# Other durations in the estimate by which a decoder-layer kernel orders its TensorE work

## The chip, the cores and the metric

The kernel runs on one core of one Trainium2 chip. The metric is device time of one execution in microseconds (us), the median of three runs. The engines are PE (TensorE, with PEld for its weight loads), DVE (VectorE), ACT (ScalarE), POOL (GpSimd) and SP (SyncE), which here only issues DMAs.

## The reference, cut to what matters

One decoder layer on x of 2048 tokens by 1024 channels, all in float32. D_FF is 2816.

```python
h = rms_norm(x, attn_norm)
dn_qkv, dn_z, dn_b, dn_a, sq, sk, sv, gate_raw = split_combined(h @ w_in)
y_dn = gated_deltanet_branch(dn_qkv, dn_z, dn_b, dn_a, ...)    # 4 heads of 128, a state carried along the tokens
y_swa = sliding_window_branch(sq, sk, sv, ...)                 # 8 query heads of 64, window 128
gates = sigmoid(gate_raw)
merged = gates[0] * (y_dn @ w_branch_dn) + gates[1] * (y_swa @ w_branch_swa)
x = x + merged @ w_out
h2 = rms_norm(x, ffn_norm)
x = x + (silu(h2 @ w_gate) * (h2 @ w_up)) @ w_down
```

Inside the first branch each chunk of tokens needs a unit triangular solve and then a step of the recurrence `S = g S + k_dec^T v_new`, so chunk follows chunk.

## The kernel before, in words

The tokens go in four blocks of 512 (`NB = 4`). A block passes through a *mixer* (projections of the delta-rule heads, gates, both branches, merge), then the output projection, then the feed-forward part. The products with weights are the **dense** work. Each is done as three matmuls (`mm3`, `tok_mm`, lines 194 and 208): both factors are split into a high and a low part of type float32r, and high x high, high x low and low x high are added in PSUM. One such triple is called a **group** below; its matmuls write tiles named `acc`. All else is **side** work: small matmuls and transposes into tiles named `aux`, with chains of operations on DVE, ACT and POOL between them. Products of the delta rule are plain float32 matmuls.

PE's order is written out by hand (`manual_schedule` for PE alone, line 1034); the framework orders the other engines by itself, side work with raised priority (line 243). `drive` (line 217) emits it: the dense work is one generator, and each side chain is a generator in `self.sides`. After every group `drive` looks for a side chain whose *due* time has come by an estimated clock `est.now`, and emits its next step, that is, the step's matmuls and what follows them on the other engines up to the next `yield`. A side step's new due time is the estimated end of the operations it emitted plus HOP + SLACK, 220 + 30 ns (line 250).

The estimate is `Estimate.note` (line 72). Every emitted operation gets a start, the latest of `est.now`, the engine's own free time, and the ready times of its inputs plus HOP (220 ns, an input made on the same engine included), and an end by a formula for its engine and size (lines 78 to 85). A matmul advances `est.now` to its end; operations on the other engines only move that engine's free time. One call of `matmul` or `transpose` is priced once. `n` is the number of columns for PE and the largest number of elements per partition for the others. `bank` (line 68) holds a side step back until the oldest of eight PSUM banks is estimated free. The splitting of weights into high and low parts (`weights`, line 155; done in block 0 only, kept in DRAM for the rest) is emitted past the estimate.

When the dense generator yields a condition, `drive` emits side steps alone, in order of their due times, until the condition holds (line 229). One such place is in `mixer`: after the gates and `branch` for all eight m, `yield lambda: len(ydn) == NH` (line 986) holds back `merge` until the last delta-rule head is done.

The four heads run in two lanes (`dn_cores`, line 710): heads 0 and 2 in one, 1 and 3 in the other. `dn_core` (line 716) of one head and block has these steps: `gu` on POOL; the decay matrix, 8 plain products and the DVE chain to `be` (lines 729 to 772); a loop of 30 small DVE operations that solves 16 x 16 blocks (line 780; the *solver loop*), which ends in `R`; two levels of three steps and three more steps that widen the solve to 128; then four chunks of three *scan steps* (lines 831 to 851, tiles `vb`, `wv`, `state` and `O`); then the norm of the output (lines 853 to 860, with 14 small DVE operations on tile `dst`; the *last wait*), the transposes of `O`, and `ydn`. When `branch` is emitted, `norm1` of the next block is started as another side chain (line 983).

Of the kernel before, what the change touches and what calls it, by code (L numbers as in the profile page):

```python
# [56 lines left out]
class Estimate:  # L57
# [14 lines left out]
    def note(self, eng, name, args, kw):  # L72
        aps = [(k, a) for k, a in list(enumerate(args)) + list(kw.items()) if hasattr(a, "tensor")]
        outs = [a for k, a in aps if k in ("out", "accum_out", 0) and (k or "out" not in kw)]
        ins = [a for k, a in aps if not any(a is o for o in outs)]
        n = max(int(np.prod([d[1] for d in list(a.ap)[1:]])) for _, a in aps)
        start = max([self.now, self.free.get(eng, 0.0)] + [self.ready.get(a.tensor.name, 0.0) + HOP for a in ins])
        if eng == "tensor":
            n = int(np.prod([d[1] for d in list(outs[0].ap)[1:]]))
            f32 = any(a.dtype == F32 for a in ins)  # L80
            end = start + max(n / 2.4 * (1 if not f32 else 2 if name == "transpose" else 4), 107 if f32 or n > 64 else 53)
            self.now = end
        else:
            end = start + {"vector": 70 + n / 0.96, "scalar": 160 + n / 1.4, "gpsimd": 100 + n * 2.2}[eng]
            self.free[eng] = end
            self.done = max(self.done, end)
        for a in outs:
            self.ready[a.tensor.name] = end
        for a in outs + ins:
            if a.tensor.name in self.banks or eng == "tensor" and a is outs[0]:  # L90
                self.seq += 1
                self.banks[a.tensor.name] = (self.seq, end)
                if len(self.banks) > 8:
                    self.banks.pop(min(self.banks, key=lambda k: self.banks[k][0]))
# [1034 lines left out]
```

## Time and profile before

| | |
|---|---|
| runs | 3184.16, 3185.84, 3180.29 us |
| median | 3184.16 us |
| profiled execution, its own time | 3183.98 us |
| its span, first to last instruction | 3182.2 us |
| granted TensorE clock over the span | 0.991 of full |
| PE busy | 3088.4 us, 97% |
| DVE, ACT, POOL busy | 44%, 26%, 13% |
| plain 512-column float32r matmul, start to start in a run of 30 | 0.235 us |

Matmul ends are modelled and matmuls overlap, so durations of single PE records are longer than what each adds; the distance from start to start tells the cost. A plain float32 matmul of the program leaves two records on PE, a float32r one or a transpose leaves one: the program has 64 calls that write `aux` from `wv` and `kd`, and the trace has 128 records of them.

### The profile page before, as it was taken

How to read it: one execution, taken by the hardware profiler on the slowest of the kernel's cores; microseconds unless marked ns; L12 is line 12 of the kernel's file. 1: busy time of each engine (PE TensorE's matmuls, PEld its weight loads, DVE VectorE, ACT ScalarE, POOL GpSimd, SP SyncE). 2: the span in 40 equal slices, each digit the busy share in tenths (PEclk: the TensorE clock that was granted, in tenths of full speed). 3: DMA queues.
4: the chain of work that ended last, by engine and by line, in shares of the span. 5: the costliest groups of instructions: out<-in, count | busy, mean ns of one | idle time of the engine just before them, and what ended most of it. 6: DMA issues, size and time to landing. Idle time of an engine off the chain costs nothing. (4 is left out here: it accounts for less than half of the span.)

```text
span 3182.2 us, 39714 instructions
## 1 busy us (share of the span) xinstructions
PE 3088.4 (97%) x14854; PEld 2520.7 (79%) x14854; DVE 1401.6 (44%) x3599; ACT 834.3 (26%) x2106; POOL 409.6 (13%) x395
## 2 busy tenths in 40 slices
PE   7889999999999999999999999999999999999999
PEld 6667778788888888778887888877888888878887
DVE  6876656533346544532216465353211655422121
ACT  4444434523323322320002323141000233110000
POOL 1423212322221100010002010011000211000000
PEclk9989999999999999999999999999999999999999
DMA  7445576688874456445566445545656544555555
GB/s 263 157 146 188 190 264 202 197 284 283 284 240 139 133 162 205 151 156 188 185 192 196 135 140 183 176 155 165 196 188 207 165 131 131 197 162 194 190 188 184
DMA packets 291848, 595.99 MB, mean 187 GB/s; under 512 B 18975, under 2 KB 20168, under 8 KB 291656
## 3 DMA queue, kind: packets, MB, share of 16 engines
q1 hardware_dynamic: 277072, 568.15, 54.4%
q10 hardware_dynamic: 14584, 25.30, 2.3%
q8 instruction: 117, 1.92, 0.2%
q14 instruction: 75, 0.61, 0.1%
HBM read 459.08 MB, written 134.30 MB: 186 GB/s over the span
## 5 line engine op out<-in xcount | busy, mean ns | idle before, releaser
L109 PE MATMUL acc<-h,whl 128*128 128x512 f32 x7296 | 1761.9, 397 | 6.2 <-DVE QE L109 6.2
L109 PEld LDWEIGHTS acc<-h,whl 128*128 128x128 f32 x7296 | 1355.8, 189 | 309.2 <-DVE QE L109 6.4
L109 PE MATMUL acc<-whl,a 128*128 128x512 f32 x2112 | 493.7, 393 | 0.0
L109 PEld LDWEIGHTS acc<-whl,a 128*128 128x128 f32 x2112 | 395.5, 188 | 90.3
L109 DVE TENSOR_TENSOR x<-x,acc 128x512 f32<-128x512 f32 x192 | 131.2, 687 | 391.3 <-PE acc L109 388.7
L173 POOL TENSOR_TENSOR whl<-wraw,whl 128x512 fp32r<-128x512 f32 x117 | 159.2, 1361 | 589.7 <-ACT whl L170 544.4
L170 ACT ACTIVATE whl<-wraw 128x512 fp32r<-128x512 f32 (+1 forms) x240 | 149.4, 629 | 295.2 <-PE acc L109 169.6
L109 DVE TENSOR_TENSOR th<-th,acc 128x512 f32<-128x512 f32 x88 | 60.4, 687 | 315.8 <-PE acc L109 315.5
L109 DVE SCALAR_TENSOR_TENSOR th<-th,acc 128x512 f32<-128x512 f32 x88 | 60.4, 687 | 307.8 <-ACT th L109 307.8
L109 PE MATMUL acc<-whl,mt 128*128 128x512 f32 x768 | 181.6, 398 | 5.4 <-DVE h L109 4.6
L109 ACT ACTIVATE th<-acc 128x512 f32<-128x512 f32 x88 | 52.6, 598 | 501.5 <-PE acc L109 501.4
L109 PEld LDWEIGHTS acc<-whl,mt 128*128 128x128 f32 x768 | 146.2, 191 | 40.1 <-DVE h L109 5.1
L109 DVE SCALAR_TENSOR_TENSOR cv<-xr,cst_sb,cv 128x512 f32<-128x512 f32 x144 | 134.4, 933 | 57.1 <-ACT cv L109 52.5
L109 ACT ACTIVATE a<-th 128x512 fp32r<-128x512 f32 x88 | 55.5, 631 | 346.7 <-DVE th L109 332.1
L173 DVE TENSOR_TENSOR whl<-wraw,whl 128x512 fp32r<-128x512 f32 (+1 forms) x123 | 94.0, 765 | 106.9 <-ACT whl L170 102.5
L109 PE MATMUL acc<-whl,h 128*128 128x264 f32 (+1 forms) x768 | 139.0, 340 | 0.0
L109 PEld LDWEIGHTS acc<-whl,h 128*128 128x128 f32 x768 | 118.0, 188 | 15.6
L109 POOL COPY ccar<-xr 128x3 f32<-128x3 f32 x48 | 9.7, 203 | 847.1 <-ACT xr L109 847.0
L109 PE MATMUL acc<-sp,whl 128*128 128x512 f32 x384 | 101.3, 405 | 0.0
L109 POOL TENSOR_TENSOR pT<-pT,cst_sb 128x512 f32<-128x512 f32 x62 | 81.9, 1351 | 130.2 <-ACT pT L109 114.2
L109 ACT ACTIVATE L<-L,ast 128x256 f32<-128x256 f32 (+1 forms) x192 | 83.5, 458 | 52.6 <-DVE ast L109 52.4
L109 PE MATMUL acc<-ydn,whl 128*128 128x512 f32 x384 | 92.2, 399 | 0.4
(186 smaller groups left out, 2808.4 us busy)
## 6 DMA issues: line engine op xcount, KB each, us to landing
whl<-wk SPq DMA_DIRECT2D x708, 512.0 KB, 3.9
wk<-whl SPq DMA_DIRECT2D x236, 512.0 KB, 3.7
wraw<-in_w_all SPq DMA_DIRECT2D x118, 512.0 KB, 4.9
x<-in_x ACTq DMA_DIRECT2D x60, 256.0 KB, 5.3
out<-x ACTq DMA_DIRECT2D x32, 256.0 KB, 3.1
whl<-wk SPq DMA_DIRECT2D x12, 528.0 KB, 4.7
wk<-whl SPq DMA_DIRECT2D x4, 528.0 KB, 4.6
wraw<-in_w_skv SPq DMA_DIRECT2D x2, 528.0 KB, 5.8
```

The lines of the kernel that those rows point to most:

```text
L109: r = f(*args, **kw)
L170: nc.scalar.activation(hi, r, AF.Copy)
L173: eng.tensor_tensor(out=lo, in0=r, in1=hi, op=ALU.subtract)
```

## The change

Four formulas of `Estimate.note` are replaced: PE's (float32r and float32, with matmul and transpose of float32 no longer told apart) and those of DVE, ACT and POOL. HOP, SLACK and everything else stay. No instruction is added or removed; what can differ is the order on PE, and with it the order that the framework gives the other engines.

```diff
         if eng == "tensor":
             n = int(np.prod([d[1] for d in list(outs[0].ap)[1:]]))
             f32 = any(a.dtype == F32 for a in ins)
-            end = start + max(n / 2.4 * (1 if not f32 else 2 if name == "transpose" else 4), 107 if f32 or n > 64 else 53)
+            end = start + (max(n * 0.452, 60) if not f32 else max(n * 0.87, 60))
             self.now = end
         else:
-            end = start + {"vector": 70 + n / 0.96, "scalar": 160 + n / 1.4, "gpsimd": 100 + n * 2.2}[eng]
+            end = start + {"vector": 155 + n * 1.04, "scalar": 150 + n * 0.92, "gpsimd": 100 + n * 2.45}[eng]
             self.free[eng] = end
             self.done = max(self.done, end)
```

In ns, by these formulas:

| operation | before | after |
|---|---|---|
| group of three 512-column float32r matmuls | 640 | 694 |
| float32 transpose, 128 columns | 107 | 111 |
| plain float32 matmul, 128 columns, one call | 213 | 111 |
| DVE, 512 elements | 603 | 687 |
| DVE, 4 elements | 74 | 159 |
| ACT, 512 elements | 526 | 621 |
| ACT, 128 elements | 251 | 268 |
| POOL, 512 elements | 1226 | 1354 |

## Rows read from the trace of the kernel before

**Rows 1.** The page, first part: busy us, share of the span, instructions.

```profile
PE 3088.4 (97%) x14854; PEld 2520.7 (79%) x14854; DVE 1401.6 (44%) x3599; ACT 834.3 (26%) x2106; POOL 409.6 (13%) x395
```

**Rows 2.** Windows of four stretches; columns in the first line.

```profile
core 0: us, PE busy (x) PEld busy (x) DVE busy (x) ACT busy (x) POOL busy (x), PEclk, DMA share, GB/s
0.00:410.00 410.00, 349.13 (x1818) 283.51 (x1819) 283.81 (x780) 184.60 (x498) 122.35 (x113) 0.95 0.55 188
1184.00:1958.00 774.00, 767.05 (x3717) 627.41 (x3715) 319.64 (x867) 173.98 (x466) 62.12 (x69) 1.00 0.53 171
393.25:405.70 12.45, 3.10 (x19) 2.34 (x18) 9.23 (x41) 6.87 (x23) 1.44 (x1) 0.67 0.47 152
1206.00:1217.00 11.00, 8.68 (x48) 7.33 (x47) 10.54 (x19) 5.97 (x10) 0.00 (x0) 0.84 0.71 221
```

**Rows 3.** Waits of PE, 80 to 410 us: us in total, times, longest.

```profile
PE aux L109 <- ACT T L109: 15.8, 3, 9.8
PE aux L109 <- DVE O L109: 9.0, 2, 7.6
```

**Rows 4.** Waits of PE, 500 us to the end, same columns.

```profile
PE aux L109 <- DVE be L109: 6.7, 9, 0.9
...
PE acc L109 <- DVE h L109: 4.6, 2, 2.3
```

**Rows 5.** PE at the end of block 1's mixer: start, us, operation.

```profile
1176.82 7.20 PE L109 MATMUL acc<-sp,whl 128*128 128x512 f32 x30
1183.86 0.60 PE L109 MATMUL aux<-cst_sb,O 128*128 128x128 f32 x4
```

**Rows 6.** Groups of operations: count | busy us, mean ns | idle before.

```profile
L109 DVE TENSOR_TENSOR x<-x,acc 128x512 f32<-128x512 f32 x192 | 131.2, 687 | 391.3 <-PE acc L109 388.7 <-DMA whl<-wk 2.1
...
L109 PE MATMUL aux<-state,cv 128*128 128x128 f32 x256 | 39.4, 277 | 0.6 <-DVE state L109 0.6
...
L109 PE MATMUL aux<-cst_sb,cv 128*128 128x128 f32 x192 | 29.6, 278 | 2.9 <-DVE cv L109 2.9
...
L109 DVE SCALAR_TENSOR_TENSOR dst<-dst 128x4 f32<-128x4 f32 x112 | 23.5, 210 | 3.4
```

**Rows 7.** DVE, end of a solver loop in block 1: start, us, operation.

```profile
1072.19 0.17 DVE L109 TENSOR_TENSOR rtmp<-bb,rr 128x4 f32<-128x4 f32 x1
1072.39 0.17 DVE L109 TENSOR_TENSOR rr<-rr,rtmp 128x4 f32<-128x4 f32 x1
1072.59 0.69 DVE L109 TENSOR_TENSOR R<-rr,blk 128x512 f32<-128x512 f32 x1
```

**Rows 8.** Chain that ended last, 12 plain records: start, us, what.

```profile
2684.16 1.34 PE aux L109 x12
```

**Rows 9.** PE around that solver loop: start, us, operation.

```profile
1065.23 12.73 PE L109 MATMUL acc<-h,whl 128*128 128x512 f32 x54
1077.80 0.38 PE L109 MATMUL aux<-cst_sb,R 128*128 128x128 f32 x2
```

**Rows 10.** Dense PE work of block 1's mixer, 965.2 to 1183.7 us.

```profile
L109 PE MATMUL acc<-h,whl 128*128 128x512 f32 x588 | 149.1, 402 | 0.0
L109 PE MATMUL acc<-sp,whl 128*128 128x512 f32 x96 | 25.0, 403 | 0.0
```

**Rows 11.** DVE at the end of block 1's mixer.

```profile
1181.47 0.69 DVE L109 TENSOR_TENSOR O<-O,dst 128x512 f32<-128x512 f32 x1
```

**Rows 12.** PE at the end of block 0's mixer, idle before in brackets.

```profile
394.33 0.71 PE L109 MATMUL aux<-state,cv 128*128 128x128 f32 x4 [0.59 <-DVE state L109]
395.49 0.49 PE L109 MATMUL aux<-vb,R 128*128 128x128 f32 x2 [0.44 <-DVE vb L109]
396.66 0.49 PE L109 MATMUL aux<-wv,kd 128*128 128x128 f32 x2 [0.69 <-ACT wv L109]
...
405.00 1.11 PE L109 MATMUL aux<-cst_sb,O 128*128 128x128 f32 x4 [7.63 <-DVE O L109]
405.77 3.97 PE L109 MATMUL acc<-ydn,whl 128*128 128x512 f32 x12
```

## The prediction

> **What bounds the kernel now.** The first part of the page has PE busy for 97% of the span and every other engine under half of it [rows 1]. No instruction is added or taken away, so PE's own work stays, and the change can only move the time in which PE stands still, 3182.2 - 3088.4 = 94 us. The windows show where it lies: PE is busy for 349 of 410 us in the first block, and for 767 of 774 us in a later one [rows 2]. The waits of PE say on what. In block 0 they are few and long: on T, copies that ACT makes late, and on O at the end of the mixer [rows 3]. From 500 us on they are short: nine on `be`, none over 0.9 us, and two on `h` at the start of an output projection [rows 4]. All that can be won is in these, and it stands against new waits that another order makes.
>
> **The change part by part: prices.** A group costs 640 ns by the old formula, 694 by the new. In a run of 30 matmuls the trace has one start every 0.235 us, 0.70 for a group [rows 5]: the new price is right, the old one 8% low. For DVE with 512 elements 687 is the trace's mean to the ns, and for 4 elements 159 stands against a mean of 210 that holds stretched ones [rows 6]. But HOP is still added between two operations of one engine. In the solver loop an operation follows the one that it needs after 0.20 us [rows 7]. The old price of such a link is 220 + 74 = 294 ns, the new one 379: 45% too long becomes 90%. The Trainium skill, "VectorE: DVE Perf Modes", section "The DRAIN you can't avoid", says that a semaphore between VectorE operations costs nothing beyond the flush of the pipeline; by it HOP within DVE would be 0, and the trace agrees, with 0.20 us from start to start for records of 0.17 us.
>
> The plain float32 matmul goes the other way. The trace has 256 records for `state`, where the program makes 128 calls (4 heads, 4 blocks, 4 chunks, 2 products); a transpose has one record for each call, 192 for 48 times 4 [rows 6]. Twelve plain records take 1.34 us [rows 8], so a record costs 0.11 us and a call 0.22. The old formula charged 213 ns, the new one charges 111: the cost of a record, half of the call's. The Trainium skill, "FP8 and Floating Point Precision", section "TensorE Precision Notes", says that true FP32 takes four passes through the array; by it the old factor of 4 was right and 0.87 ns a column is not, which speaks against this line of the change, as the records do.
>
> **The change part by part: the chain of a lane.** By the formulas I work out the wait behind each step of one `dn_core` with nothing else in the way, in ns and in groups. `be` step: 5,720 / 640 = 8.9 groups, then 7,310 / 694 = 10.5. Solver loop: 11,500, 17.9, then 14,190, 20.4. Last wait: 5,980, 9.3, then 7,310, 10.5. The old numbers can be seen in PE's order: 54 matmuls, 18 groups, behind the solver loop [rows 9], and 30, 10 groups, in the last wait [rows 5]. Steps with one 512- or 128-wide operation (T, W, R, scan steps) come to 1.1 to 1.7 groups by both and take two, as now. One core grows by 1.6 + 2.5 + 1.2 = 5.3 groups or 3.6 us, and a lane has two cores in a row: 7.2 us.
>
> A side product of the other lane helps to fill a due time only by its price. In block 1 some 84 plain products of lane 0 lie in lane 1's waits (44 of 128 columns in each core, nearly two cores). Each counted 213 of its 222 ns and now counts 111, so lane 1 comes later by 84 x 0.10 = 8.6 us.
>
> The third term no row shows: the estimate keeps one free time per engine, so lane 1's DVE operations are booked behind lane 0's solver loops (2.7 us longer), last waits (1.3) and `be` steps (1.6). At least nothing of it reaches lane 1; at most all of it from two cores, 11 us. I take 5, nearer to the lower end, because a lane that is late itself has less to wait out. Sum: lane 1 ends 7.2 + 8.6 + 5 = 21 us later against the dense work (16 to 27).
>
> **What the lane ends against.** The mixer has a fixed stock of dense work, in block 1 684 matmuls, 228 groups, from head 1's start to the last branch matmul [rows 10]. After it `drive` has only side steps until `ydn` is complete. In block 1 O's transposes follow the last of these matmuls at once [rows 5]; O was ready at 1182.2 [rows 11], 1.7 us before PE came. Blocks 2 and 3 repeat this pattern. So 1.7 us are to spare, and of 21 us nearly all is uncovered: steps that PE does one by one, as in block 0 already now, after waits of 0.59, 0.44 and 0.69 us, and then 7.63 us until O [rows 12].
>
> A scan step in its place takes two groups and 1.7 calls, 1.40 + 0.37 = 1.77 us. Of 21 us, 11 groups or 7.6 us are the last wait, and the rest is 8 of the 12 scan steps. Idle: 8 x 0.57 = 4.6 us, and for the last wait 5.3 us (block 1's own chain, 1176.8 to 1182.2 [rows 5, 11]) to 7.6 (block 0 [rows 12]). In block 0's end the granted clock was 0.67 [rows 2], so PE had gone from 2.4 to 1.2 GHz as it stood; the 12 matmuls behind it took 3.97 us where 11 x 0.235 + 0.39 = 3.0 would do, and O's transposes 1.11 for 0.60 [rows 5, 12], 1.4 us in all. Together 11.3 to 13.6; I take 12.5 in each of blocks 1 to 3, 37.5 us. At 16 us: 5 steps, 2.7 + 5.3 + 1.4 = 9.4, three times 28. At 27 us: 11 steps, 6.3 + 7.6 + 1.4, and products at half clock, 0.37 in some four of them, 16.8: three times 50.
>
> **What is won.** The `be` waits of blocks 1 to 3 go, since that step comes 1.6 groups (1.1 us) later and none is over 0.9: -7 us [rows 4]. The two waits on `h` (4.6 us [rows 4]) come from transposes of the next block that fall due just as the merge ends; with the lane late they fall inside the merge, as in block 0. With the half clock around them (granted 0.84 over 11 us, 1.75 us lost each [rows 2]) that is -8 us. Block 0: its end takes 21 us of chain more, 12 steps at 0.57: +7. Its other long waits, some 30 us [rows 2, 3], hang on how ACT and DVE mix weight splits, which the estimate doesn't see, with side work. Later steps shorten them by 0 to 25 us; I take 9, since a due time that is a group later meets such a queue only by chance.
>
> Total: 37.5 - 7 - 8 + 7 - 9 = +21 us. The profiled execution took 3183.98 us, its span and 1.8 us around it, and lies within 0.2 us of the median. So 3205 us. Ends: 28 - 7 - 8 + 7 - 25 = -5 and 50 - 7 - 8 + 7 = +42, or +50 if the waits on `h` stay: 3179 to 3234.
>
> **The rivals.**
> *The chain still fits.* If rounding to groups swallows the growth, so that lane 1 ends under 2 us behind the branch work, no new wait opens: -7 of `be`, -13 in block 0, 3164 us. For it: the work as executed has slack (0.20 us a link against 294 priced). Against it: due times, not slack, set PE's order, and block 1 ends with no group to spare [rows 5]. It decides at a shortage of 2 us.
> *The order hardly moves.* The change doesn't do what it says: most prices grow together (687 / 603 = 1.14, 694 / 640 = 1.08), most steps keep their two groups, and a shortage of some 8 us, the last wait alone, 6.7 us a block, is paid by `be`, `h` and block 0: 20 - 15 - 5 = 0, 3184 us. Against it: the halved plain products, which no other price follows.
> *More than that.* Lane 1 is so late that its widening steps fall behind the dense work too: over 3240 us.
>
> **How the numbers follow.** Forecast 0.66 (of it 0.06 within 0.2% of before), chain fits 0.17, order hardly moves 0.13, more 0.04. 0.2%, about 6 us, is what a measurement of this kernel can tell from no change. Faster: 0.17 and 0.02 of the third, 0.19. Same: 0.06 + 0.11 = 0.17. Slower: 0.60 + 0.04 = 0.64. The range takes the forecast's own ends, some of the last case and half of the first rival: 3166 to 3238.
>
> **What would show it.** In the profile after: PE waits on O once a block, 5 us or more in blocks 1 to 3, with `state`, `vb` and `wv` products ahead of it that have no dense matmuls between them; no waits on `be`; 63 matmuls where 54 follow the solver loop now; a lower granted clock at the ends of three more mixers. I am wrong if branch matmuls still lie between the last scan steps and O in blocks 1 to 3, or if block 0 alone changes by more than 20 us.

## The result, and the profile after

The changed kernel takes 3274.1 us (median of four executions, 3270.6 to 3278.3), the kernel before on the same chip 3183.4 (3180.3 to 3185.8). The ratio is 1.0286, interval 1.0268 to 1.0304: 91 us slower. The forecast was 3205 us, in a range of 3166 to 3238. The direction was right, the size was not: 21 us foretold, 91 measured.

The first line of the page after (engine, busy us, share, instructions), against [rows 1]:

```profile
PE 3129.7 (96%) x14854; PEld 2549.8 (78%) x14854; DVE 1402.9 (43%) x3599; ACT 837.3 (26%) x2106; POOL 405.4 (12%) x395
```

The instructions are the same in number. PE's busy time rose by 41.3 us, and what is left of the span, 3273.3 - 3129.7 = 143.6 us against 93.8, by 49.8. So less than half of the loss is work that takes longer, and the rest is PE standing still. Both lie at the ends of the mixers. The windows of the changed kernel from the last branch matmul to the first merge matmul of each block, the **tails** (columns in the first line):

```profile
core 0: us, PE busy (x) PEld busy (x) DVE busy (x) ACT busy (x) POOL busy (x), PEclk, DMA share, GB/s
360.00:437.00 77.00, 42.95 (x233) 34.98 (x232) 42.51 (x139) 25.44 (x72) 6.17 (x5) 0.69 0.13 45
1194.00:1235.00 41.00, 22.18 (x127) 17.62 (x126) 24.55 (x81) 17.77 (x57) 0.00 (x0) 0.72 0.20 64
1990.00:2033.00 43.00, 24.74 (x131) 20.35 (x129) 24.73 (x81) 18.70 (x57) 0.00 (x0) 0.66 0.20 62
2788.50:2821.00 32.50, 18.62 (x97) 14.47 (x96) 13.89 (x52) 8.32 (x33) 0.00 (x0) 0.66 0.05 17
```

Before, the tail of block 0 was 12.9 us [rows 12] and each of the others 0.6, O's transposes alone [rows 5]. Now they make 194 us, in which PE is idle for 85 and runs at a mean granted clock of 0.66 to 0.72 of full, so part of the time at the lower of its two levels, 1.2 instead of 2.4 GHz. Part of block 1's tail on PE (start, us, operation, idle before and its releaser in brackets):

```profile
1193.15 0.93 PE L109 MATMUL acc<-sp,whl 128*128 128x512 f32 x3
1193.92 0.61 PE L109 MATMUL aux<-state,cv 128*128 128x128 f32 x4
1194.37 1.06 PE L109 MATMUL aux<-R,W 128*128 128x128 f32 x8
...
1197.81 0.67 PE L109 MATMUL aux<-T,B 64*64 64x64 f32 x8
...
1203.29 0.49 PE L109 MATMUL aux<-wv,kd 128*128 128x128 f32 x2 [0.59 <-ACT wv L109]
...
1209.21 1.11 PE L109 MATMUL aux<-cst_sb,O 128*128 128x128 f32 x4 [5.20 <-DVE O L109]
...
1213.63 4.77 PE L109 MATMUL aux<-cst_sb,x 128*128 128x128 f32 x19 [2.46 <-DVE x L109]
...
1225.95 1.22 PE L109 MATMUL aux<-state,cv 128*128 128x128 f32 x4 [0.44 <-DVE state L109]
...
1234.65 1.09 PE L109 MATMUL aux<-cst_sb,O 128*128 128x128 f32 x4 [4.66 <-DVE O L109]
1235.39 2.06 PE L109 MATMUL acc<-ydn,whl 128*128 128x512 f32 x4
```

Behind the last branch matmul stand the last scan steps of head 2, O of head 2, the x transposes of `norm1`, and of head 3 the last four widening steps (from the `R,W` line on), all scan steps and O. Four `state` products take 0.61 us at the start, before the clock fell, and 1.22 at the lower clock. The waits of PE from 500 us to the end (us in total, times, longest), against [rows 4]:

```profile
PE aux L109 <- DVE O L109: 28.1, 6, 5.2
PE aux L109 <- DVE x L109: 7.6, 4, 2.5
PE aux L109 <- ACT wv L109: 5.4, 13, 0.6
...
PE aux L109 <- DVE vb L109: 4.7, 10, 0.5
...
PE aux L109 <- DVE state L109: 2.6, 6, 0.4
```

O waits twice a block, not once. The nine waits on `be` and the two long ones on `h` are gone. In block 0 (80 to 440 us), against [rows 3], the waits on T fell by 8.4 us, and one of 5.8 on POOL's `be` is new, beside one on x in the tail:

```profile
PE aux L109 <- DVE O L109: 8.7, 2, 4.6
PE aux L109 <- ACT T L109: 7.4, 3, 3.1
PE aux L109 <- DVE x L109: 7.1, 1, 7.1
PE aux L109 <- POOL be L109: 5.8, 1, 5.8
```

### The profile page after: what moved, and what is told of

It is laid out like the page before. It is cut to its first block, busy times and chain, and to the rows that moved or that the text cites. A ratio compares the mean times of both kernels' runs of the same rounds, so it can differ in the third digit from the quotient of the medians.

```text
span 3273.3 us, 39753 instructions
## 1 busy us (share of the span) xinstructions
PE 3129.7 (96%) x14854; PEld 2549.8 (78%) x14854; DVE 1402.9 (43%) x3599; ACT 837.3 (26%) x2106; POOL 405.4 (12%) x395
## 4 chain that ended last, share of the span: by engine, by line
PE 85%; DVE 4%; ACT 2%; POOL 1%; issue 1%; DMA 0%; ACTq 0%; POOLq 0%; DVEq 0%
PE acc L109 74%; PE aux L109 11%; DVE dst L109 1%; ACT jk L109 0%; POOL pT L109 0%; DVE qT L109 0%; DVE O L109 0%; ACT L L109 0%; DVE spw L109 0%; DMA whl<-wk 0%; DVE state L109 0%; POOL gu L109 0%; DVE x L109 0%; DVE vb L109 0%; DVE L L109 0%
## 5 line engine op out<-in xcount | busy, mean ns | idle before, releaser
L109 DVE SCALAR_TENSOR_TENSOR cv<-xr,cst_sb,cv 128x512 f32<-128x512 f32 x144 | 126.7, 880 | 70.6 <-ACT cv L109 68.1
```

Source lines behind the costliest of these rows:

```text
L109: r = f(*args, **kw)
```

## The experiments

The theory on record: lane 1 comes late against a fixed stock of dense work, by its own longer chain (7.2 us), by the halved plain products (8.6) and by bookings on the one VectorE queue of the estimate (5 of at most 11). The rival that the tails suggested: the bookings are nearly all of it. Tails and block times are read from PE's rows as above: a tail from the last branch matmul to the first merge matmul, a block from first merge matmul to first merge matmul (block 0 from the start). All in us, blocks 0 / 1 / 2 / 3; medians, and ratios to the kernel before on the same chip with their intervals. The spans of the profiles lie 0 to 7 us below the medians.

| kernel | median | ratio | tails | blocks |
|---|---|---|---|---|
| before | 3183.4 | | 12.9 / 0.6 / 0.6 / 0.6 | 405.8 / 778.4 / 774.2 / 774.2 |
| the change | 3274.1 | 1.0286 (1.0268 to 1.0304) | 77.5 / 41.7 / 43.0 / 32.8 | 437.3 / 798.1 / 797.6 / 788.3 |
| e1_only_pe | 3209.4 | 1.0080 (1.0065 to 1.0095) | 14.5 / 0.2 / 0.2 / 0.2 | 404.2 / 786.4 / 785.2 / 784.8 |
| e1_only_halved | 3216.0 | 1.0101 (1.0086 to 1.0116) | 47.5 / 14.8 / 14.3 / 13.5 | 415.9 / 783.7 / 781.6 / 780.9 |
| e1_vec_slope | 3187.3 | 1.0011 (1.0002 to 1.0020) | 31.8 / 1.0 / 1.0 / 1.0 | 416.8 / 772.7 / 772.8 / 773.1 |
| e1_no_queue | 3485.5 | 1.0950 (1.0932 to 1.0968) | 0.2 / 0.2 / 0.2 / 0.2 | 442.3 / 868.5 / 863.4 / 859.2 |
| e2_hop_same | 3190.2 | 1.0020 (1.0010 to 1.0029) | 7.0 / 0.2 / 0.2 / 0.2 | 392.7 / 788.8 / 779.0 / 778.2 |
| e2_f32_two | 3242.9 | 1.0187 (1.0172 to 1.0203) | 50.8 / 29.9 / 30.8 / 19.0 | 419.5 / 794.1 / 794.6 / 783.0 |
| e2_norm1_later | 3275.8 | 1.0292 (1.0275 to 1.0309) | 67.3 / 32.8 / 32.8 / 32.8 | 425.8 / 800.6 / 798.7 / 797.1 |
| e2_warm | 3291.6 | 1.0339 (1.0323 to 1.0354) | 80.3 / 48.5 / 46.8 / 32.3 | 440.5 / 805.8 / 802.1 / 786.2 |
| e3_lanes | 3250.7 | 1.0216 (1.0200 to 1.0231) | 59.5 / 32.9 / 31.9 / 20.9 | 421.8 / 796.7 / 795.3 / 783.7 |
| e3_chains | 3240.7 | 1.0185 (1.0168 to 1.0202) | 0.2 / 0.2 / 0.2 / 0.2 | 406.2 / 800.2 / 792.9 / 791.1 |
| e3_same60 | 3173.4 | 0.9970 (0.9961 to 0.9979) | 6.3 / 0.2 / 0.2 / 0.2 | 393.7 / 779.2 / 774.4 / 774.2 |
| e3_f32_two_same120 | 3180.1 | 0.9988 (0.9979 to 0.9998) | 15.1 / 0.2 / 0.2 / 0.2 | 400.7 / 777.4 / 773.9 / 773.8 |

### One price at a time

**The PE line alone** (the rest as before):

```diff
-            end = start + max(n / 2.4 * (1 if not f32 else 2 if name == "transpose" else 4), 107 if f32 or n > 64 else 53)
+            end = start + (max(n * 0.452, 60) if not f32 else max(n * 0.87, 60))
```

> The change's PE line alone: the group at 694 ns, the plain product at 111, but the old prices of DVE, ACT and POOL. My prediction's theory: the halved plain products are the largest single term (8.6 of 21 us of lateness in each of blocks 1 to 3), and without the longer DVE chains some 7 us of shortage stay after the spare 1.7: about 6 us of uncovered steps a block, 3195 to 3205 us. Rival, the engine prices make the lateness and the dearer group (640 to 694) buys slack that outweighs the halved products: no side step behind the branch work of blocks 1 to 3, no be waits added, 3170 to 3188 us.

Measured 3209.4, 4 us above my theory's bracket. The number is near, the mechanism is not: in blocks 1 to 3 no tail opens, PE's last O stands ahead of the last branch matmul. The time is lost in waits for other tiles:

```profile
PE aux L109 <- DVE cv L109: 11.9, 9, 2.5
PE aux L109 <- DVE R L109: 8.4, 3, 3.1
PE aux L109 <- DVE L L109: 7.6, 7, 2.4
PE aux L109 <- ACT L L109: 6.2, 6, 2.1
```

Before, `cv` had 2.9 us of waits, `R` 1.8 and `L` 3.1. How I read it: with the group at 694 ns and VectorE still at its old prices, fewer matmuls are put between two side steps, and the steps come before their inputs. So there are two ways to lose: too late, a tail; too early, short waits. The prediction knew only the first.

**The halved product alone:**

```diff
-            end = start + max(n / 2.4 * (1 if not f32 else 2 if name == "transpose" else 4), 107 if f32 or n > 64 else 53)
+            end = start + max(n / 2.4 * (1 if not f32 else 2), 107 if f32 or n > 64 else 53)
```

> One term of the prediction by itself: the kernel before, with the plain float32 product charged 2 cycles a column instead of 4 (107 ns for 128 columns in place of 213); the group stays at 640 and the engines at their old prices. Prediction's term: lane 1 comes 8.6 us later against the dense work; about 5 us of uncovered steps a block plus block 0, 3198 to 3210 us, with O's transposes behind 3 to 5 uncovered scan steps in blocks 1 to 3. Rival, the term is nothing because PE's order follows due times only: 3180 to 3188 us.

Measured 3216.0, above my theory's bracket. The mechanism is the predicted one; block 1's end on PE:

```profile
1184.19 0.95 PE L109 MATMUL acc<-sp,whl 128*128 128x512 f32 x3
...
1186.18 0.71 PE L109 MATMUL aux<-state,cv 128*128 128x128 f32 x4 [0.59 <-DVE state L109]
...
1198.82 1.12 PE L109 MATMUL aux<-cst_sb,O 128*128 128x128 f32 x4 [5.39 <-DVE O L109]
```

After the branch work there are uncovered scan steps and 5.4 us until O. But the tail grew by 13 to 14 us, where 8.6 of lateness less 1.7 spare were to give 7. The same price undone within the change:

```diff
-            end = start + (max(n * 0.452, 60) if not f32 else max(n * 0.87, 60))
+            end = start + (max(n * 0.452, 60) if not f32 else max(n * 0.87, 60) * (1 if name == "transpose" else 2))
```

> All of the change, but a plain float32 product is charged two records (222 ns for 128 columns), what the trace shows, instead of one. The prediction's second term, 8.6 us of lateness in a block, is thereby taken out of the changed kernel. If the terms add: tails between the last branch matmul and the merge of about 33 us in blocks 1 and 2 and 20 to 24 in block 3 (41.7, 43.0 and 32.8 with the change), at the 0.46 us that each us of tail costs there some 4 us a block and as much in block 0: 3252 to 3264 us. Rival: the queue on VectorE decides alone and the halved products are covered by it: the tails stay at 40 and more, 3268 to 3278 us.

Measured 3242.9, below both brackets. The tails shrink by 26.7, 11.8, 12.2 and 13.8 us. Blocks 1 to 3 give back 4.0, 3.0 and 5.3, as expected there; block 0 gives back 17.8. So this line is worth 12 to 14 us of tail in each of blocks 1 to 3, where the term had 8.6 of lateness, and about a third of the loss. The Trainium skill, "FP8 and Floating Point Precision", section "TensorE Precision Notes", which says that true FP32 takes four passes, was weighed in the prediction against this line. The run agrees: with the call at two records, 222 ns where the trace has 0.22 us, the kernel is 31 us faster than the change.

**VectorE's constant undone:**

```diff
-            end = start + {"vector": 155 + n * 1.04, "scalar": 150 + n * 0.92, "gpsimd": 100 + n * 2.45}[eng]
+            end = start + {"vector": 70 + n * 1.04, "scalar": 150 + n * 0.92, "gpsimd": 100 + n * 2.45}[eng]
```

> The change with one number undone: VectorE's constant stays 70 ns (slope 1.04, and all other new prices stay). My prediction's theory: the 8.6 us of the halved products stay and the growth of the chains shrinks to the slope's, so shortage of some 9 us a block stays, 3200 to 3215 us. Rival (queue): the 85 ns on each of the small VectorE operations is what makes the lanes late, because the estimate keeps one queue for VectorE and books whatever is emitted later, of the other lane and of the dense work, behind a whole solver loop; then blocks 1 to 3 end as in the kernel before (only O's transposes behind the branch work), and what is left is block 0: 3180 to 3200 us.

Measured 3187.3, the rival's. With this one number back at 70, 87 of the 91 us are gone, though the halved product, the dearer group and the ACT and POOL prices stay. Blocks 1 to 3 are 1 to 6 us faster than before, with a tail of 1.0, O's transposes alone; block 0 is 11 us slower. The 85 ns on each small VectorE operation are thus the condition of the loss. Whether they act through each lane's own chain or through the bookings, this run doesn't tell.

### Own chain or bookings

**No queue at all:**

```diff
-        start = max([self.now, self.free.get(eng, 0.0)] + [self.ready.get(a.tensor.name, 0.0) + HOP for a in ins])
+        start = max([self.now] + [self.ready.get(a.tensor.name, 0.0) + HOP for a in ins])
```

> All of the change's prices, but the estimate no longer keeps a free time for VectorE, ScalarE and GpSimd: an operation's start is the latest of the clock and of its inputs. My prediction's theory: the queue was a term of 5 us in 21, so most of the loss stays, 3240 to 3265 us. Rival (queue): the lateness is that of the queue, no side step is left behind the branch work in any block, O's transposes lie inside it, and the loss of 91 us is gone in blocks 1 to 3 at the least: 3160 to 3195 us, where steps that now come earlier than their inputs may give some waits of PE on DVE tiles.

Measured 3485.5: the tails are gone, as the rival said, and its time is missed by 290 us. PE now waits for inputs of the projections' side chains:

```profile
PE aux L109 <- DVE cv L109: 85.9, 41, 8.8
PE aux L109 <- DVE L L109: 59.9, 16, 6.6
```

Both theories had the queue as a mere source of lateness. It is also what keeps steps from coming too early.

**The other lane's bookings apart** (the prediction's third term by itself; an operation of one lane no longer starts behind the other lane's):

```diff
-        start = max([self.now, self.free.get(eng, 0.0)] + [...])
+        other = {0: 1, 1: 0}.get(self.lane)
+        start = max([self.now] + [t for (e, l), t in self.free.items() if e == eng and (l is None or l != other)] + [...])
...
-            self.free[eng] = end
+            self.free[eng, self.lane] = end
```

> All of the change's prices; in the estimate an operation of one delta-rule lane is no longer booked behind operations of the other lane on DVE, ACT and POOL (it still is behind those of the dense work and of all other side chains). This is the prediction's third term, which it put at 5 us of lateness, 11 at most. If that size was right, the tails between the last branch matmul and the merge shrink from 41.7, 43.0 and 32.8 us by 11 at most. If the other lane's bookings were most of the lateness, they are gone. In the order that this kernel emits, 56 of 86 side calls stay behind the branch work of blocks 1 and 2: so I expect tails of about 30 us there and 20 in block 3, 3235 to 3255 us, which would say that the larger part of the lateness is booked behind neither the own chain nor the other lane.

Measured 3250.7, tails 32.9, 31.9 and 20.9: 9 to 12 us shorter than with the change, as expected. So the third term, as far as it speaks of the other lane, is 9 to 12 us of tail, not 5, and that is a lower bound: an operation of the dense work or of another side chain still starts behind both lanes, and each lane behind it.

**Every side chain's bookings apart** (a chain sees its own and the dense work's):

```diff
+        start = max([self.now] + [t for (e, l), t in self.free.items() if e == eng and (l is None or self.chain is None or l == self.chain)] + [...])
...
+            self.free[eng, self.chain] = end
```

> All of the change's prices; in the estimate every side chain (the two lanes, the posts of the projections, the sliding window, the norms) has its own free times on DVE, ACT and POOL, shared with the dense work only. If the lateness of the lanes is bookings behind other side chains, no tail is left in any block, the core of head 1 in block 1 takes 75 to 100 us from its gu products to its O transposes (155 with the change, 134 before), and the loss has another form: steps before their inputs, waits of PE on cv, L and R as without any queue. Time then between 3230 and 3480 us, since only the bookings across chains are gone. If the lateness were the growth of the own chains and the halved products, as the prediction's first two terms say (16 of 21 us), tails of 25 us and more would stay.

Measured 3240.7, with no tail in any block. All prices are the change's, own chain and halved products included; only the direct bookings behind other chains are gone, and all of the lateness with them. But those that the kernel before had are gone too, so the run shows what such bookings come to in all, not what the change added to them. PE's rows of head 1 in block 1, `gu` products and O transposes; first the kernel before:

```profile
969.42 0.63 PE L109 MATMUL aux<-gu,slr 128*128 128x512 f32 x2
...
1103.05 0.60 PE L109 MATMUL aux<-cst_sb,O 128*128 128x128 f32 x4
...
1107.51 0.73 PE L109 MATMUL aux<-gu,slr 128*128 128x512 f32 x2
```

The third line is head 3's start; its O is at 1183.86 [rows 5]. The changed kernel, the same three lines (O of head 3 at 1234.65, above):

```profile
995.82 0.63 PE L109 MATMUL aux<-gu,slr 128*128 128x512 f32 x2
...
1150.32 0.60 PE L109 MATMUL aux<-cst_sb,O 128*128 128x128 f32 x4
...
1153.91 0.71 PE L109 MATMUL aux<-gu,slr 128*128 128x512 f32 x2
```

And with the chains apart, with head 3's O as fourth line:

```profile
986.62 0.71 PE L110 MATMUL aux<-gu,slr 128*128 128x512 f32 x2
...
1076.34 0.60 PE L110 MATMUL aux<-cst_sb,O 128*128 128x128 f32 x4
...
1124.69 0.71 PE L110 MATMUL aux<-gu,slr 128*128 128x512 f32 x2
...
1201.03 0.60 PE L110 MATMUL aux<-cst_sb,O 128*128 128x128 f32 x4
```

Head 1's core takes 133.6 us before, 154.5 with the change and 89.7 with the chains apart, so far less than before the change. Head 3's takes 76.4, 80.7 and 76.3; it starts later, when the posts of the projections are past, before and with the change with head 2's core beside it for most of the time. Its 80.7 us do not measure its own chain, since half of them lie in the tail: in block 3 the same core takes 71.8. The dense matmuls that PE does meanwhile tell more. Head 1's core, from its `gu` products to its O, before and with the change:

```profile
L109 PE MATMUL acc<-h,whl 128*128 128x512 f32 x414 | 104.4, 401 | 0.0
```
```profile
L109 PE MATMUL acc<-h,whl 128*128 128x512 f32 x522 | 130.3, 400 | 0.0
```

That is 138 groups and 174, 36 more or 25 us; with the chains apart it is 78. The waits that replace the tail in this run are short ones, `cv` 20.3 us in 12, `vb` 11.6, `qT` 10.7, `R` 9.8: too early again.

**The link within one engine priced as measured** (30 ns instead of HOP, so 189 for a solver link where the trace has 0.20 us [rows 7]):

```diff
+SAME = 30
...
-        start = max([self.now, self.free.get(eng, 0.0)] + [self.ready.get(a.tensor.name, 0.0) + HOP for a in ins])
+        start = max([self.now, self.free.get(eng, 0.0)] + [self.ready.get(a.tensor.name, 0.0) + (SAME if self.by.get(a.tensor.name) == eng else HOP) for a in ins])
...
+            self.by[a.tensor.name] = eng
```

> All of the change's prices, but an input made on the same engine is ready 30 ns after its end instead of 220 (HOP stays between engines, and the one queue per engine stays too). A solver link is then priced 159 + 30 = 189 ns, and the trace has 200. Theory: the lanes are late because each small VectorE operation carries 159 + 220; with the link priced right nothing is left behind the branch work in any block and the steps are not early either: 3170 to 3195 us. Rival: the dear link stood in for VectorE's other work, which the estimate books too short or not at all, so steps now come before their inputs, as with the PE line alone: waits of PE on cv, L and R of 20 us and more, the last O before the last branch matmul, 3200 to 3260 us.

Measured 3190.2: within the theory's 3170 to 3195, and 6 us slower than before. The tails of blocks 1 to 3 are gone and block 0 is 13 us faster than before, but blocks 1 to 3 lose 10, 5 and 4 us. A part of that is to be seen on PE: O of head 1, in each of the three blocks in this form, is asked for 4 us too early:

```profile
1085.13 1.11 PE L112 MATMUL aux<-cst_sb,O 128*128 128x128 f32 x4 [4.17 <-DVE O L112]
```

So the rival has a share. That a link dearer than its own time had covered what the estimate books too short fits this, but is argued.

### What the tail is made of

**norm1 later:**

```diff
+        yield lambda: len(ydn) == NH
         if b + 1 < self.nblocks:
             nxt = []
             self.spawn(self.norm1(b + 1, nxt))
         else:
             nxt = None
-        yield lambda: len(ydn) == NH
```

> The changed kernel, but norm1 of the next block is started when ydn is complete instead of when branch is emitted; nothing else. Its 32 x transposes then leave the tails of blocks 0 to 2, where those of block 1 stand for 7.7 us with 4.4 us of waits on x. Theory: they lengthen the tail, PE does one thing at a time there: 12 to 24 us less, 3250 to 3262 us, with tails of some 35 us in blocks 1 and 2 against 33 in block 3, which has no norm1. Rival: PE waits in the tail for head 3's chain anyway and the transposes only fill the gaps: tails stay within 2 us of 41.7 and 43.0, 3268 to 3280 us; or more, up to 3290, if h then comes late for the next projections.

Measured 3275.8, as the rival's time, but not for its first reason. The tails of blocks 1 and 2 do get 9 to 10 us shorter, so that all of blocks 1 to 3 have 32.8, and the time comes back behind them, by the late `h` that the rival named second: the last matmul of block 1's output projection starts at 1305.7 us (1303.5 with the change), and the waits on `h` ahead of dense matmuls that the change had removed are back, 6.9 us in two. The x transposes in the tail are no loss of their own; their work and their waits only lie in another place.

**PE kept busy in the tail** (two matmuls more ahead of each side step there):

```diff
+                        if getattr(self, "warm", False):
+                            fill = self.aux()
+                            for _ in range(2):
+                                self.raw.tensor.matmul(fill, self.slr, self.slr.unsqueeze(1).broadcast_to([P, NT, P]),
+                                                       start=True, stop=True)
                         self.side_step(min(self.sides, key=lambda x: x[1]))
```

> The changed kernel with two added 512-column float32r matmuls on constants, into a bank that nothing reads, ahead of each side step between the last branch matmul and the merge. They keep PE busy in the gaps. Theory 1: the lower granted clock at the ends of the mixers is a part of the loss (products of 0.37 us instead of 0.22): the clock stays at 2.4 GHz there, and each of the four tails is 2 to 4 us shorter, 3258 to 3268 us. Theory 2: the tail is a chain of ACT and DVE steps and the clock of PE is no part of it: within 4 us of 3274. Theory 3: the fillers stand in the way of steps that are ready, 0.47 us for each of some 30 steps: up to 14 us a block more, 3280 to 3320 us.

Measured 3291.6, 17 us slower than the change. The clock came back; block 3's tail, columns as above:

```profile
2802.00:2834.00 32.00, 25.39 (x147) 18.18 (x145) 13.77 (x52) 8.76 (x33) 0.00 (x0) 1.00 0.05 17
```

At full clock and with 50 matmuls more this tail is as long as without them (32.3 and 32.8 us); those of blocks 1 and 2 are 7 and 4 us longer. The fillers take what the clock gives, and more where `norm1` is in the tail too. They also take one of the eight PSUM banks each time, and whether that holds steps up was not tried. How much the lower clock alone costs, this run doesn't separate; the time is in theory 3's bracket.

### Between late and early

Two kernels with all of the change's prices and a dearer link than 189 ns. The first sets `SAME = 60` (219 ns for a solver link):

> All of the change's prices, with an input from the same engine ready 60 ns after its end (220 with the change, 30 in the run that had no tail in blocks 1 to 3 and 6 us too much there). A link of the solver loop is then priced 219 ns, where the trace has 200. Theory, too late and too early cost both: the lanes come nearer to the end of the branch work, waits of PE on cv, L and O get fewer, blocks 1 to 3 take 773 to 778 us each and block 0 some 393: 3168 to 3182 us, the first version below the kernel before. Rival, the order around one value is as good as any other: 3186 to 3195.

Measured 3173.4, in the theory's bracket: 11 us (0.3%) faster than before, with an interval clearly below 1. It keeps block 0's gain (393.7) and block 1's O of head 3 just ahead of the branch work's end:

```profile
1164.81 2.26 PE L112 MATMUL acc<-sp,whl 128*128 128x512 f32 x9
1166.91 0.60 PE L112 MATMUL aux<-cst_sb,O 128*128 128x128 f32 x4
1167.26 5.79 PE L112 MATMUL acc<-sp,whl 128*128 128x512 f32 x24
```

The waits of 4 us on O in each of blocks 1 to 3 are gone with 30 ns more on a link. The second prices a plain product at two records as well and sets `SAME = 120`:

> All of the change's prices, a plain float32 product charged two records (222 ns), and an input from the same engine ready 120 ns after its end: a solver link is priced 279 ns, near the 294 of the kernel before, and every single price is a measured one. In its order nothing but O's transposes stays behind the branch work in blocks 1 to 3, and 11 side calls in block 0. Theory: prices that are right for single operations, with a link that leaves room for what the estimate doesn't see, give the order of the kernel before or a better one: 3165 to 3185 us, blocks 1 to 3 at 772 to 776 us each. Rival: its lanes end up to 10 us ahead of the branch work, so that steps are early and PE waits on cv and O as with the link at 189 ns: 3186 to 3200.

Measured 3180.1, 0.12% faster (0.02 to 0.21), the theory's bracket too: blocks 1 to 3 as before, block 0 5 us faster. Neither has every price right: the first halves the plain product, the second charges 279 ns for a link that takes 200. What the two share is that the lanes of blocks 1 to 3 end just ahead of the branch work's end. That this place decides, and not each single price, is argued from the two.

## Why the prediction was right in direction and wrong in size

**What held.** PE's work and the end of the mixer were the place. The `be` waits went, the two `h` waits went, 63 matmuls follow the solver loop where 54 did:

```profile
1128.65 14.74 PE L109 MATMUL acc<-h,whl 128*128 128x512 f32 x63
```

Tails opened in blocks 1 to 3, with `state`, `vb` and `wv` products one by one, long waits on O, and a lower clock. The two rivals on the fast side are refuted: there was neither a chain that fits nor an order that hardly moves. What came is the third rival, at 0.04: "Lane 1 is so late that its widening steps fall behind the dense work too: over 3240 us." T's waits in block 0 fell by 8.4 where 9 were taken off its long waits, but others came there, on `be` and on x.

**The step that failed** is the lateness, 21 us (16 to 27), and in it above all the third term: "at least nothing of it reaches lane 1; at most all of it from two cores, 11 us. I take 5". PE's order tells how late lane 1 became. In block 1 of the changed kernel the branch work is over when head 3 is at the `R,W` products of 1194.37 (above). Before, these products, and the dense matmuls that were still to come behind them:

```profile
1144.19 1.05 PE L109 MATMUL aux<-R,W 128*128 128x128 f32 x8
```
```profile
L109 PE MATMUL acc<-sp,whl 128*128 128x512 f32 x96 | 25.0, 403 | 0.0
L109 PE MATMUL acc<-h,whl 128*128 128x512 f32 x36 | 9.7, 408 | 0.0
```

So lane 1 is 132 matmuls late, 44 groups or 31 us of dense work; PE's order in blocks 2 and 3 is the same. 5 groups of it are there when head 1's core starts, for which the prediction had nothing. 36 come in head 1's core, for which its three terms make some 15. From head 3's start to its `R,W` products only 3 more come, where the own chain of these steps was put at 1.6 + 2.5.

The term counted as booked ahead only the other lane's loops, waits and `be` steps. The estimate books *every* VectorE operation of *every* chain in one queue in the order of emission, and one that must wait for its input keeps the queue closed for all emitted behind it, ready or not. The 85 ns thus act on each such link of the posts, the sliding window and the lanes, and reach head 1's core, which runs beside them all, many times over. The runs, in us of tail in blocks 1 to 3: 9 to 12 by the other lane at the least (e3_lanes), nothing left without the direct bookings behind any other chain (e3_chains), nothing but O's transposes without the 85 ns (e1_vec_slope). These figures overlap, with the halved products' 12 to 14 too: each is what goes when one part is undone, and they add to more than the whole, which fits a lane that is late only by what exceeds its slack. But the bound of 11 left out the chains beside the two lanes, and without their bookings the rest of the tail goes. What is left to bookings in head 1's core can be estimated. With the plain product at two records (e2_f32_two) the core still takes 163 groups:

```profile
L109 PE MATMUL acc<-h,whl 128*128 128x512 f32 x489 | 123.2, 401 | 0.0
```

That is 25 more than before; the own chain was worked out as 5.3, and some 20 groups or 14 us remain, where the third term had 2.5 for a core and 5.5 at most.

The trace of before could have warned of it. Head 1's core took 138 groups there and head 3's 80 for the same instructions, so up to 58 groups, 41 us, of head 1's core hung on what ran beside it. A rise of the booked prices (a solver link by 29%) put on these too would have been an estimate of 0.29 x 41 = 12 us for this core, where the second and third terms had 7 for it. That is nearer, but still short of what came: 36 groups less 5.3 of its own chain, 21 us.

**What a tail costs** was too low as well. The prediction paid 12.5 us in each of blocks 1 to 3: some 11 of idle time and 1.4 of clock. (It turned all 21 us of lateness into steps, the 1.7 us to spare included; that is half a microsecond a block.) In block 3, whose tail holds the lanes alone, PE was idle for 13.9 us, and for 16.3 it was busy at the lower clock:

```profile
2799.03:2826.33 27.30, 16.25 (x50) 12.56 (x51) 11.01 (x40) 4.58 (x16) 0.00 (x0) 0.50 0.00 0
```

A `state` product takes twice as long at this level, so half of it, 8 us, is an estimate of what the clock took there; in the same way it is 7 and 10 in and just behind the tails of blocks 1 and 2, and 14 in block 0. Over the four tails, 194 us, PE was idle for 85. Its busy time rose by 41.3 over the whole span, and by this estimate 38 of that are the clock's (39, less the 1.4 of the kernel before at block 0's end). Outside the tails idle time fell by 26 us (93.8 less 9.4 at block 0's end [rows 2], against 143.6 less 85.0), where the won terms, `be`, `h` and block 0, had been put at 7, 4.6 without the clock, and 9. 85.0 - 9.4 - 26 + 41 is the 91 us.

**The halved products** were 12 to 14 us of tail a block where the term had 8.6. Why the tail grows by more than the count of 84 calls gives was not tried.

**Block 0** was put at +7 - 9 and came to +31.5, so it met the condition set for being wrong. Its tail went from 12.9 to 77.5 us, not by 21. Head 1's O, with 189 dense matmuls (63 groups, 44 us) between it and the end of the branch work before, now comes behind all of them, so lane 1 is later there than in the other blocks. The same prices make it: the tail is 31.8 with the old constant, 50.8 with the plain product at two records, 0.2 with the chains apart. The +7 also had nothing for the clock. Over the kernels with tails there, block 0's time roughly follows the tail: from 392.7 at 7.0 (e2_hop_same) to 437.3 at 77.5, 0.63 us for each.

So 70 us were missing: 33.5 in block 0, and nearly all of the rest in blocks 1 to 3, by lateness of 31 us where 21 was put, more yet in block 0, and by the clock.

**What stays open:** which of the chains beside the lanes books the most, how exactly the lateness divides among the three terms, why lane 1 is so much later in block 0, and what the lower clock costs by itself, beyond the estimate.

## What to carry to other kernels

When an estimate orders the work, a truer price need not give a better order: a price can stand in for what the estimate doesn't see, so change a price together with its companions (here the constant of an operation and the hop on the same engine), and look at both sides, tails (late) and waits ahead of inputs (early). Before sizing a change of prices, compare in the trace how much dense work the same chain takes with few and with many chains beside it: what it takes more may hang on the others, and a change of the queue's prices acts on that too.

## What the hardware showed that was not expected

Work in a tail is not only uncovered but slower: the mean granted clock was 0.66 to 0.72 there, four `state` products took 1.22 us at the lower level instead of 0.61, and PE's busy time rose by 41 us for the same 14854 matmuls. Matmuls on constants brought the clock to 0.91 to 1.00 in the tails of blocks 1 to 3, and the kernel was 17 us slower with them.
